# One more product step between the parts of a token tile's norm and transpose, in the out projection and the values of a Hymba layer

## The chip, the cores and the metric

The kernel runs on one core of a Trainium2 chip. Times are device microseconds (us) of one execution of the whole layer, lower is better. The core's engines are TensorE (PE, matrix products), VectorE (DVE), ScalarE (ACT), GpSimd (POOL) and SyncE (SP, which here only issues DMA transfers); each has its own instruction stream and runs it in order, and they meet through semaphores.

## The reference

The reference is one layer of a streaming encoder in float32, with 2048 tokens of width 1024. The pieces that lie around the change, cut to the core:

```python
y = concat([ya, yh]) @ w_out            # out projection
h = x + rms_norm(y, g_mix_post)         # h1
u = rms_norm(h, g_x_pre)
s = (u @ wq) . (m @ wk); p = softmax(s) # 4 heads, 256 memory tokens
y = (p . (m @ wv)) @ wo                 # values and output projection
h = h + rms_norm(y, g_x_post)           # h2
u = rms_norm(h, g_ffn_pre)
h = h + rms_norm((silu(u @ w_gate) * (u @ w_up)) @ w_down, g_ffn_post)
```

`rms_norm(a, g)` is `a / sqrt(mean(a*a) + eps) * g`, over the 1024 channels of a token.

## The kernel before

A first part of the kernel computes the in projection, the sliding window attention and the recurrence. After it, `phases()` (L1191) runs a list of jobs: the out projection, the scores, the values (in which the memory's value projection and the output matrix have been multiplied together beforehand), two jobs for the hidden half of the feed-forward network (FFN, for the first and second half of the tokens) and three for its down projection. In the out projection, the scores and the values a job is a row of eight blocks, and a block is two token tiles, n and n+1, of 128 tokens each. A block is one matrix product in the manner of Strassen: `seven` (L1114) makes it from seven product steps (numbered p = 1, 2, 5, 6, 7, 3, 4), each of which is twelve matmuls of 128x128 by 128x512: four pieces of the inner dimension times three (L1110 high part by high part, L1111 high by low, L1112 low by high). The first two and the last two blocks of a job are interleaved in pairs, step by step; the four between run alone. So the whole of `phases()` is one long row of product steps.

Each product step needs two operands as pairs of a rounded high part and a remainder: S, made from the tokens (`streamed`, `split2`: ACT or POOL rounds at L974 or L976, DVE subtracts at L977), and T, made from the weights or, for the FFN, from the norm's result (L974 with L977 on 128x1024). S is made about two steps ahead. T of the next job is loaded and split in halves, one half for each step.

After a step, results leave the banks of the accumulator: ACT copies (`part`, L1125; `row`, L1477) or DVE adds (L1475), and ACT squares each half with a sum (L1453). After the last step of a block, its token tiles' tail begins, written as a generator (`after()`, then `rest()`): at every product step that is issued, each live generator runs on to its next `yield`. So a `yield` is a distance of one product step in the program. The tail of a block of the values runs:

1. the reciprocal root of the mean square (`rstds`, POOL L1464, L1466, L1468), the scale by it and the gain (DVE L1584), a DMA on POOL that adds the residual to the row in place (`add`, L1482), and the store of the row to `h2_d` (SP, L78), one token tile per yield;
2. the squares of the sum (`mean_squares`, ACT L1453, called twice per tile), one tile per yield, and `rstds`;
3. the norm (DVE L1605) into a new row tile u, one tile per yield;
4. eight 128x128 transposes per tile on PE (L1364, into two banks), each half copied back into the row by ACT (L1365), and the store to `u_d`;
5. for tiles 4 to 7, sums and differences with the rows of the tiles 0 to 3 that are read back from `u_d`: one load `o`, four DVE operations (L1620, L1621, L1624, L1625) and four stores to `u_s` per tile. They become T of the FFN.

In the out projection (scale L1500) the tail is the same with the input x as residual, `h1_d`, no norm (its factor goes into the scores) and the transposes written in place over the row. For the last two blocks of a job (n of 12 or more) `rest()` runs beside the next job, on rows that are read back.

The Python order is not the order on the engines. A scheduler places every instruction, and may issue one ahead of where it was written, if its inputs allow. `behind()` (L1037) binds what is written inside it: it is issued after the last instruction that ACT, DVE, PE and SP each had when the current product step was written (`mark`, L1045). All row tiles (y, u, o, the sums, and the loads for T) share one ring of nine buffers (`row_tile`, L1435), and all loads and all stores of this part go through SP's one stream, in order: where an issue waits, those behind it wait as well.

## Time and profile before

| | us |
|---|---|
| median of 3 runs (lowest, highest) | 2555.17 (2553.72, 2556.72) |
| the profiled execution, its own time | 2553.45 |
| its span, first to last instruction | 2551.7 |
| PE busy in it | 2508.4 |
| DVE busy | 1759.2 |
| ACT busy | 1250.0 |
| POOL busy | 465.4 |

The profiled execution lies 1.72 us under the median. The out projection takes the stretch from 770 to 936 us of the span, the scores reach to 1102, the values to 1277, and the FFN's first product step follows there. Nearly all work on the other engines lies beside PE; where PE has a gap, the profile names what it waited for.

### The profile page before, as it was taken

The page shows a single profiled execution, that of the slowest core. Times are in us where ns is not written, and L with a number is a line of the kernel's source. Part 1 is how long each engine was busy: PE and PEld are TensorE (multiplying, and loading weights), DVE is VectorE, ACT ScalarE, POOL GpSimd, SP SyncE. Part 2 cuts the span into 40 slices and gives each one's busy share as a digit, 9 for nine tenths or more (in the row PEclk, how much of TensorE's full clock was granted, in tenths as well). Part 3 has the DMA queues.
Part 4 walks back from the last instruction along what each step waited for, and adds up shares of the span by engine and source line. Part 5 has one row for each costly group of instructions (what it writes and reads, how often), then busy time and mean ns, then how long its engine had stood idle before and what let it go on. Part 6 is the DMA issues. An engine that isn't in the chain of part 4 may idle for free.

```text
span 2551.7 us, 34118 instructions
## 1 busy us (share of the span) xinstructions
PE 2508.4 (98%) x12012; PEld 2091.8 (82%) x12012; DVE 1759.2 (69%) x2813; ACT 1250.0 (49%) x2606; POOL 465.4 (18%) x641
## 2 busy tenths in 40 slices
PE   8999999999999999999999999999999999999998
PEld 6777888887998888888788888888888888888886
DVE  6868588788667587787875655586666566664756
ACT  5454365556555566565554333353333344533543
POOL 2233343222323343224210000000000000000022
PEclk9999999999999999999999999999999999999999
DMA  6264545465996795858974542254555433666798
GB/s 239 97 209 133 176 142 164 153 200 186 283 310 225 217 281 198 283 194 241 313 229 129 180 146 75 99 182 141 182 197 193 161 129 131 206 208 196 221 226 206
DMA packets 269386, 489.97 MB, mean 192 GB/s; under 512 B 20640, under 2 KB 127136, under 8 KB 268704
## 3 DMA queue, kind: packets, MB, share of 16 engines
q1 hardware_dynamic: 255680, 439.57, 51.5%
q0 software_dynamic: 12384, 45.09, 8.9%
q10 hardware_dynamic: 1152, 3.15, 0.3%
q8 instruction: 94, 1.54, 0.2%
q14 instruction: 76, 0.62, 0.1%
HBM read 326.26 MB, written 161.48 MB: 191 GB/s over the span
## 4 chain that ended last, share of the span: by engine, by line
PE 89%; DMA 3%; DVE 2%; issue 2%; ACT 2%; POOL 1%; SPq 0%; POOLq 0%; DVEq 0%; ACTq 0%
PE psm L1110 23%; PE psm L1112 23%; PE psm L1111 23%; PE psg L170 3%; PE psg L172 3%; PE psg L171 3%; PE pss L1364 1%; DMA row<-h_d 1%; PE pss L824 0%; PE pst L824 0%; DMA sraw<-y_d 0%; PE psh L870 0%; PE psh L170 0%; PE psh L171 0%; PE psh L172 0%
## 5 line engine op out<-in xcount | busy, mean ns | idle before, releaser
L1110 PE MATMUL psm<-T,S 128*128 128x512 f32 x2744 | 1063.5, 392 | 12.1 <-ACT part L1125 5.4
L1111 PE MATMUL psm<-T,S 128*128 128x512 f32 x2744 | 1070.8, 390 | 0.0
L1112 PE MATMUL psm<-T,S 128*128 128x512 f32 x2744 | 1063.3, 391 | 3.2 <-DVE S L977 3.1
L1110 PEld LDWEIGHTS psm<-T,S 128*128 128x128 f32 x2744 | 516.0, 188 | 123.9 <-ACT part L1125 8.0
L1112 PEld LDWEIGHTS psm<-T,S 128*128 128x128 f32 x2744 | 516.0, 188 | 113.5 <-DVE S L977 5.7
L1111 PEld LDWEIGHTS psm<-T,S 128*128 128x128 f32 x2744 | 516.2, 188 | 106.2
L974 ACT ACTIVATE S<-sum 128x512 fp32r<-128x512 f32 (+1 forms) x336 | 206.2, 618 | 327.2 <-PE psm L1112 326.1
L977 DVE TENSOR_TENSOR S<-sraw,S 128x512 fp32r<-128x512 f32 (+1 forms) x312 | 211.7, 686 | 210.1 <-ACT S L974 195.0
L977 DVE TENSOR_TENSOR S<-sum,S 128x512 fp32r<-128x512 f32 (+1 forms) x400 | 271.6, 684 | 83.1 <-ACT S L974 65.5
L1125 ACT ACTIVATE part<-psm 128x512 f32<-128x512 f32 x294 | 173.1, 592 | 184.4 <-PE psm L1112 180.2
L974 ACT ACTIVATE S<-sraw 128x512 fp32r<-128x512 f32 (+1 forms) x271 | 165.7, 616 | 168.4 <-PE psm L1112 153.3
L1482 POOL DMA_DIRECT2D row<-y_d x28 | 25.1, 895 | 1072.2 <-DMA sraw<-hid_d 905.3
L170 PE MATMUL psg<-u,whi 128*128 128x512 f32 x352 | 142.6, 405 | 3.9 <-DVE z L696 2.1
L1453 ACT ACTIVATE junk<-row 128x512 f32<-128x512 f32 x160 | 99.6, 625 | 92.2 <-DVE row L1475 28.9
L977 DVE TENSOR_TENSOR T<-row,T 128x1024 fp32r<-128x1024 f32 x104 | 123.2, 1192 | 28.8 <-ACT T L974 28.4
L172 PE MATMUL psg<-u,wlo 128*128 128x512 f32 x352 | 142.0, 404 | 0.5 <-DVE wlo L153 0.5
L171 PE MATMUL psg<-u,whi 128*128 128x512 f32 x352 | 141.7, 403 | 0.0
L974 ACT ACTIVATE T<-row 128x1024 fp32r<-128x1024 f32 x104 | 105.3, 1023 | 20.2 <-DMA row<-in_w_down_dram 10.4
L1657 DVE TENSOR_TENSOR part<-psm,part 128x512 f32<-128x512 f32 x66 | 45.5, 689 | 66.6 <-PE psm L1112 66.4
L153 DVE TENSOR_TENSOR wlo<-raw,whi 128x1024 fp32r<-128x1024 f32 x54 | 68.1, 1263 | 29.0 <-ACT whi L150 18.4
L976 POOL TENSOR_SCALAR S<-sum 128x512 fp32r<-128x512 f32 x64 | 52.1, 814 | 174.1 <-PE psm L1112 142.4
L1648 DVE TENSOR_TENSOR row<-psm,part 128x512 f32<-128x512 f32 x66 | 45.5, 689 | 54.6 <-PE psm L1112 54.5
(343 smaller groups left out, 3472.4 us busy)
## 6 DMA issues: line engine op xcount, KB each, us to landing
sraw<-in_w_gate_dram SPq DMA_DIRECT2D x44, 512.0 KB, 5.0
sraw<-in_w_up_dram SPq DMA_DIRECT2D x44, 512.0 KB, 4.9
hid_d<-row SPq DMA_DIRECT2D x44, 512.0 KB, 2.7
h_d<-row SPq DMA_DIRECT2D x32, 512.0 KB, 7.0
y_d<-row SPq DMA_DIRECT2D x32, 512.0 KB, 4.2
sraw<-hid_d SPq DMA_DIRECT2D x32, 512.0 KB, 5.4
row<-h_d POOLq DMA_DIRECT2D x30, 512.0 KB, 7.4
row<-y_d POOLq DMA_DIRECT2D x28, 512.0 KB, 7.5
```

Of the source, the lines that this page charges most:

```text
L153: nc.vector.tensor_tensor(lo, raw, f32(hi), ALU.subtract)
L170: nc.tensor.matmul(ps, ah, bh, start=(i == 0), stop=False)
L171: nc.tensor.matmul(ps, ah, bl, start=False, stop=False)
L172: nc.tensor.matmul(ps, al, bh, start=False, stop=(i == n - 1))
L974: self.nc.scalar.activation(hi, raw, AF.Copy)
L976: self.nc.gpsimd.tensor_scalar(hi, raw, 1.0, 1.0, ALU.mult, ALU.mult)
L977: self.nc.vector.tensor_tensor(lo, raw, f32(hi), ALU.subtract)
L1110: nc.tensor.matmul(ps, s[:, 0, k, :], t[:, 0, k, :], start=st, stop=False, **kw)
L1111: nc.tensor.matmul(ps, s[:, 0, k, :], t[:, 1, k, :], start=False, stop=False, **kw)
L1112: nc.tensor.matmul(ps, s[:, 1, k, :], t[:, 0, k, :], start=False, stop=sp, **kw)
L1125: nc.scalar.activation(t, ps, AF.Copy)
L1453: self.nc.scalar.activation(junk, a, AF.Square, scale=float(D) ** -0.5, accum_out=to)
```

## The change

A product step more stands between the parts of a tile's tail: one `yield` more before the squares, for the early blocks and for the late ones; squares and transposes are written under `behind()`, so that the scheduler can no longer issue them ahead of their step; and in the values, one `yield` more between the norm and the transposes. No instruction, no transfer and no computed value is added or taken away.

```diff
--- before.py
+++ after.py
@@ -1503,6 +1503,7 @@
                 yield
             if n < NT - 4:
                 yield
+                yield
                 yield from rest()
 
         def rest():
@@ -1510,16 +1511,19 @@
             if n >= NT - 4:
                 for i in range(2):
                     y[i] = self.rows_of(self.h1_d, n + i)
-                for _ in range(3):
+                for _ in range(4):
                     yield
             for i in range(2):
-                self.mean_squares(y[i], i, s2)
+                with self.behind():
+                    self.mean_squares(y[i], i, s2)
                 yield
             r = self.rstds(s2)
             nc.gpsimd.tensor_scalar(self.r_x[:, n:n + 2], r, 1.0, None, ALU.mult)
             yield
             for i in range(2):
-                self.store(self.h1t_d[n + i], self.transposed(y[i], y[i]))
+                with self.behind():
+                    tv = self.transposed(y[i], y[i])
+                self.store(self.h1t_d[n + i], tv)
                 yield
 
         if n >= NT - 4:
@@ -1587,6 +1591,7 @@
                 yield
             if n < NT - 4:
                 yield
+                yield
                 yield from rest()
 
         def rest():
@@ -1594,10 +1599,11 @@
             if n >= NT - 4:
                 for i in range(2):
                     y[i] = self.rows_of(self.h2_d, n + i)
-                for _ in range(3):
+                for _ in range(4):
                     yield
             for i in range(2):
-                self.mean_squares(y[i], i, s2)
+                with self.behind():
+                    self.mean_squares(y[i], i, s2)
                 yield
             r = self.rstds(s2)
             u = [self.row_tile() for _ in range(2)]
@@ -1606,8 +1612,10 @@
                 yield
             o = []
             yield
+            yield
             for i in range(2):
-                tv = self.transposed(u[i], u[i])
+                with self.behind():
+                    tv = self.transposed(u[i], u[i])
                 self.store_transposed(self.u_d, n + i, tv)
                 if 4 <= n < 8:
                     o.append(self.row_tile().rearrange("p (k t) -> p k t", k=KT))
```

What this makes of the order shows on the engines. In the rows below a row names the line, the operation, what it writes and what it reads; the lines of the changed kernel have shifted by up to eight. The first place is ACT in the out projection, about where tiles 6 to 9 are squared and tile 6 is transposed. `row_1089` is tile 6, `row_1119` tile 7, `row_1097` and `row_1123` are tiles 8 and 9. Before:

```order
L1125 ACTIVATE part_1160_8547<-psm_1140_8452 128x512
L974 ACTIVATE S_1184_8646<-sraw_1139_8450 128x512
L1453 ACTIVATE junk_1163_8554,q_s_1157_8530<-row_1119_8337 128x512
L1365 ACTIVATE row_1089_8193<-pss_1178_8611 128x512
L1453 ACTIVATE junk_1164_8556,q_s_1157_8530<-row_1119_8337 128x512
L1365 ACTIVATE row_1089_8193<-pss_1179_8617 128x512
L1453 ACTIVATE junk_1166_8559,q_s_1165_8558<-row_1097_8221 128x512
L1453 ACTIVATE junk_1167_8561,q_s_1165_8558<-row_1097_8221 128x512
L974 ACTIVATE S_1205_8741<-sum_1204_8739 128x512
L1365 ACTIVATE row_1119_8337<-pss_1185_8649 128x512
```

And now:

```order
L1453 ACTIVATE junk_1166_8573,q_s_1160_8549<-row_1119_8337 128x512
L1453 ACTIVATE junk_1167_8575,q_s_1160_8549<-row_1119_8337 128x512
L1453 ACTIVATE junk_1169_8578,q_s_1168_8577<-row_1097_8221 128x512
L1453 ACTIVATE junk_1170_8580,q_s_1168_8577<-row_1097_8221 128x512
L1453 ACTIVATE junk_1171_8595,q_s_1148_8497<-row_1149_8498 128x512
L1453 ACTIVATE junk_1176_8607,q_s_1168_8577<-row_1123_8358 128x512
L974 ACTIVATE S_1212_8783<-sum_1211_8781 128x512
L1453 ACTIVATE junk_1177_8609,q_s_1168_8577<-row_1123_8358 128x512
L1477 ACTIVATE row_1163_8566<-psm_1140_8452 128x512
L1453 ACTIVATE junk_1178_8624,q_s_1148_8497<-row_1163_8566 128x512
L1365 ACTIVATE row_1089_8193<-pss_1180_8629 128x512
L1125 ACTIVATE part_1188_8666<-psm_1187_8653 128x512
```

The copies of the transposed tile 6 back into its row (L1365) stood between the squares of tile 7, and now stand behind the squares of tiles 7, 8 and 9.

The second place is PE in the values, at the transposes of tile 8, whose normed row is `row_2010` before and `row_2011` now. The `psm` tiles are the accumulators of two product steps, one after the other; before, the transposes cut into the first of them:

```order
L1111 MATMUL psm_2031_12680<-T_1695_11081,S_2020_12631 128x512
L1364 MATMUL pss_2027_12661<-ident_77,row_2010_12580 128x128 x4
L1364 MATMUL pss_2028_12667<-ident_77,row_2010_12580 128x128 x4
L1112 MATMUL psm_2031_12680<-T_1695_11081,S_2020_12631 128x512
L1110 MATMUL psm_2040_12718<-T_1695_11081,S_2026_12658 128x512
```

Now they stand behind both of them, and the product step that follows is the next one again:

```order
L1111 MATMUL psm_2036_12692<-T_1695_11081,S_2026_12652 128x512
L1112 MATMUL psm_2036_12692<-T_1695_11081,S_2026_12652 128x512
L1364 MATMUL pss_2042_12715<-ident_77,row_2011_12595 128x128 x4
L1364 MATMUL pss_2043_12721<-ident_77,row_2011_12595 128x128 x4
L1110 MATMUL psm_2046_12733<-T_1710_11156,S_2034_12687 128x512
```

Between the norm's place and the transposes there are 13 matmuls more than before: the last of the first step and all twelve of the second.

The third place is SP, and DVE with it, in the values, where tiles 4 and 5 are combined with tiles 0 and 1. Loads of `o` read `u_d`, stores of the sums go to `u_s0`, and `h2_d` takes the rows of tiles 6 and 7. SP before (`row_1935` and `row_1942` are the two `o`, `row_1884` and `row_1904` are tiles 6 and 7):

```order
L75 DMA row_1935_12233<-u_d_65 128x8x128
L75 DMA row_1942_12271<-u_d_65 128x8x128
L75 DMA sraw_1968_12390<-pt_d_60 128x2x512
L78 DMA u_d_65<-row_1914_12142 128x8x128
L78 DMA u_s0_4509<-row_1946_12292 512x1x128 x2
L75 DMA sraw_2014_12608<-in_w_gate_dram 128x2x512
L78 DMA u_d_65<-row_1915_12143 128x8x128
L78 DMA h2_d_62<-row_1884_12000 128x1024
L78 DMA h2_d_62<-row_1904_12107 128x1024
L78 DMA u_s0_4509<-row_1935_12233 512x1x128
L78 DMA u_s0_4509<-row_1957_12347 512x1x128 x2
```

And now (`row_1948` is the second `o`; tiles 6 and 7 are `row_1882` and `row_1899`; `row_1954` and `row_1972` hold the sums of tiles 4 and 5):

```order
L78 DMA u_d_65<-row_1916_12160 128x8x128
L78 DMA h2_d_62<-row_1882_11987 128x1024
L78 DMA h2_d_62<-row_1899_12089 128x1024
L75 DMA row_1948_12309<-u_d_65 128x8x128
L78 DMA u_s0_4509<-row_1954_12334 512x1x128 x2
L78 DMA u_d_65<-row_1917_12161 128x8x128
L78 DMA u_s0_4509<-row_1942_12275 512x1x128 x2
L78 DMA u_s0_4509<-row_1972_12402 512x1x128 x2
```

The second load of `o` and the first stores to `u_s0` stood ahead of the two stores to `h2_d`, and now stand behind them.

In the same place DVE has the norms of tiles 6 and 7 (L1605), S for the next product steps (L977), and the scales of tiles 8 and 9 (L1584). It had before:

```order
L1605 TENSOR_SCALAR row_1961_12356<-row_1884_12000,q_r_1960_12354,extra_1771_11458 128x1024
L1624 TENSOR_TENSOR row_1942_12271<-row_1942_12271,row_1957_12347 128x512
L1605 TENSOR_SCALAR row_1962_12357<-row_1904_12107,q_r_1960_12354,extra_1771_11458 128x1024
L1079 TENSOR_TENSOR sum_2060_12794<-sum_2044_12736,sraw_1966_12386 128x512
L977 TENSOR_TENSOR S_1994_12513<-sum_1993_12511,S_1994_12513 128x512
L1625 TENSOR_TENSOR row_1942_12271<-row_1942_12271 128x512
L977 TENSOR_TENSOR S_2001_12540<-sraw_1919_12166,S_2001_12540 128x512
L1079 TENSOR_TENSOR sum_2070_12827<-sraw_1965_12384 128x512
L1475 TENSOR_TENSOR row_1978_12435<-psm_1976_12421,part_1970_12405 128x512
L1584 TENSOR_SCALAR row_1929_12211<-row_1929_12211,q_r_1975_12416,g_1770_11456 128x1024
L1584 TENSOR_SCALAR row_1950_12312<-row_1950_12312,q_r_1975_12416,g_1770_11456 128x1024
```

And now (the norm is L1611, the scale L1588, the combination L1628 and L1629):

```order
L1628 TENSOR_TENSOR row_1972_12402<-row_1917_12161,row_1948_12309 128x512
L1629 TENSOR_TENSOR row_1972_12402<-row_1917_12161 128x512
L1611 TENSOR_SCALAR row_1963_12372<-row_1899_12089,q_r_1961_12369,extra_1771_11458 128x1024
L977 TENSOR_TENSOR S_1988_12483<-sum_1987_12481,S_1988_12483 128x512
L977 TENSOR_TENSOR S_1994_12517<-sraw_1919_12165,S_1994_12517 128x512
L1475 TENSOR_TENSOR row_1978_12429<-psm_1976_12415,part_1969_12395 128x512
L1632 TENSOR_TENSOR row_1948_12309<-row_1948_12309,row_1972_12402 128x512
L1588 TENSOR_SCALAR row_1929_12211<-row_1929_12211,q_r_1975_12410,g_1770_11456 128x1024
L1588 TENSOR_SCALAR row_1943_12289<-row_1943_12289,q_r_1975_12410,g_1770_11456 128x1024
```

The combination of tile 5 into `row_1972`, which was done before this stretch, now stands at its head, ahead of the norm of tile 7, of two S and of both scales.

## The prediction

> **What bounds the kernel now.** I read first how busy each engine is in the stretches that the change touches, by windows of time.
>
> ```profile
> core 0: us, PE busy (x) PEld busy (x) DVE busy (x) ACT busy (x) POOL busy (x), PEclk, DMA share, GB/s
> 740.00:960.00 220.00, 218.33 (x1035) 180.49 (x1034) 154.28 (x198) 124.86 (x258) 76.62 (x102) 1.00 0.80 247
> 960.00:1100.00 140.00, 140.00 (x682) 116.85 (x682) 108.41 (x194) 84.01 (x204) 37.24 (x55) 1.00 0.73 247
> 1100.00:1262.00 162.00, 157.24 (x738) 129.56 (x738) 126.31 (x178) 96.01 (x219) 57.20 (x75) 0.99 0.81 240
> 1220.00:1240.00 20.00, 18.41 (x91) 15.16 (x90) 13.02 (x19) 10.88 (x29) 7.21 (x10) 1.00 1.05 304
> 1240.00:1260.00 20.00, 17.27 (x76) 13.71 (x75) 15.54 (x21) 10.98 (x25) 5.22 (x9) 0.96 1.07 319
> 1262.00:1320.00 58.00, 58.00 (x266) 48.18 (x265) 50.09 (x66) 35.33 (x60) 9.95 (x11) 1.00 0.90 285
> ```
>
> PE has no gap in the scores and none after 1262; all that can be won lies in 1.67 us of idle time in the out projection (some of it ahead of the first tail) and 4.76 us in the values. The DMA share of about 1.05 in the last two fifths of the values says that the transfers there are as dense as they get, so they land late. Then I read PE's timeline for the single waits.
>
> ```profile
> 881.79 0.40 PE L1112 MATMUL psm<-T,S 128*128 128x512 f32 x1
> 879.91 0.66 PE L1364 MATMUL pss<-ident,row 128*128 128x128 f32 x4 [0.33 <-ACT row L1365]
> 882.50 0.50 PE L1110 MATMUL psm<-T,S 128*128 128x512 f32 x1 [0.31 <-ACT part L1125]
> 1174.13 0.50 PE L1110 MATMUL psm<-T,S 128*128 128x512 f32 x1 [0.44 <-ACT part L1125]
> 1236.84 0.39 PE L1111 MATMUL psm<-T,S 128*128 128x512 f32 x1
> 1238.83 1.06 PE L1364 MATMUL pss<-ident,row 128*128 128x128 f32 x8 [1.59 <-DVE row L1605]
> 1252.23 0.39 PE L1112 MATMUL psm<-T,S 128*128 128x512 f32 x1
> 1254.27 0.39 PE L1112 MATMUL psm<-T,S 128*128 128x512 f32 x1
> 1256.78 0.50 PE L1110 MATMUL psm<-T,S 128*128 128x512 f32 x1 [2.12 <-ACT S L974]
> 1258.12 0.54 PE L1112 MATMUL psm<-T,S 128*128 128x512 f32 x1 [0.61 <-DVE S L977]
> 1258.46 0.63 PE L1110 MATMUL psm<-T,S 128*128 128x512 f32 x1
> 1261.87 0.40 PE L1112 MATMUL psm<-T,S 128*128 128x512 f32 x1
> ```
>
> From 1252.23 to 1254.27 there are nine matmuls, 0.227 us each; that is the pace of an undisturbed step, 2.72 us for twelve. Against this pace 882.50 comes 0.48 us late, and with the 0.33 at 879.91 the out projection's transposes cost about 0.9 us. In the values the transposes of tile 8 wait 1.59 us for the norm, then one product step waits 2.12 and 0.61 us for its S, and from 1258.46 to 1261.87 eight matmuls start 0.43 us apart, which is half clock (PEclk 0.96 in that slice) and costs 8 x (0.43 - 0.227) = 1.6 us. With 0.44 us at 1174.13 all of it is 7.3 us, 0.3% of the time: the most that the change can win.
>
> What stands behind the waits of the values is the chain that ended last.
>
> ```profile
> 1198.50 0.90 POOL row L1482
> 1199.81 9.13 DMA row<-h_d
> 1222.26 11.12 DMA row<-h_d
> 1233.46 0.18 ACT junk L1453
> 1237.04 0.24 DVE row L1605
> 1244.13 1.29 DVE row L1584
> 1245.77 7.57 DMA row<-h_d
> 1253.44 1.34 ACT junk L1453 x4
> ```
>
> It is a tail feeding the next: scale (L1584), the add of the residual (L1482, 7.6 to 11.1 us until it lands), squares, norm, and on DVE the next tile's scale behind the norm. The S that PE awaits at 1256.78 is rounded by ACT right behind the squares at 1253.44, which began when the add of tile 10 had landed.
>
> **The change in the out projection.** ACT's timeline has the one long wait that the new order takes out.
>
> ```profile
> 876.33 0.60 ACT L1365 ACTIVATE row<-pss 128x512 f32<-128x512 f32 x1 [4.45 <-DMA h_d<-row]
> ```
>
> The copy of tile 6 writes over the row whose store to `h1_d` is still under way, and holds ACT's stream for 4.45 us; squares and part copies then crowd, and PE is late at 879.91 and 882.50. In the new order the squares of tiles 7 to 9 come first and the copy at least one product step (2.72 us) later, when the store has landed or nearly so. I take off 0.9 us. Bounds: nothing, if the two banks of the transposes are then late again, and 1.3 us, with one neighbouring delay of about 0.4. The wait at 1174.13 is for a part copy that stands late in both orders: unchanged.
>
> **The change in the values: the queue on SP.** These are the issues and DVE's rows that the order moves.
>
> ```profile
> 1194.12 0.98 SPq L75 DMA_DIRECT2D row<-u_d  x2
> 1206.16 3.45 SPq L78 DMA_DIRECT2D h_d<-row  x2
> 1209.70 6.67 SPq L78 DMA_DIRECT2D u_s<-row  x5
> 1207.42 0.68 DVE L1620 TENSOR_TENSOR row<-row,row 128x512 f32<-128x512 f32 x1
> 1219.43 2.47 DVE L1584 SCALAR_TENSOR_TENSOR row<-row,q_r,g 128x1024 f32<-128x1024 f32 x2
> 1233.02 0.69 DVE L1620 TENSOR_TENSOR row<-row,row 128x512 f32<-128x512 f32 x1 [4.67 <-DMA u_d<-row]
> u_s<-row SPq DMA_DIRECT2D x16, 256.0 KB, 6.3
> hid_d<-row SPq DMA_DIRECT2D x44, 512.0 KB, 2.7
> ```
>
> The stores of tiles 6 and 7 to `h2_d` can go only when the adds have landed, the second at 1199.81 + 9.13 = 1208.94, and SP is through them at 1206.16 + 3.45 = 1209.6. Before, both loads of `o` went at 1194.12. Now the second load and the stores of tile 4's sums stand behind: the load goes at 1209.6, two stores at about 1210.5 and 1211.6 (6.67 us for five, so 1.1 to 1.3 each), and with 6.3 us they have landed at about 1218. In the ring of nine rows the sums of tile 5 (`row_1972`) now get the place of the sums of tile 4, so DVE cannot combine tile 5 before 1218, where it did at 1207.42. Behind this in DVE's stream stand the norm of tile 7, two S and the scales of tiles 8 and 9. Counting DVE starts 0.6 us apart for 512 columns and 1.2 for 1024 (the rows above: two in 2.47), the two combinations, the norm, two S, an output sum and one more combination end at 1218 + 6 x 0.6 + 1.2 = 1222.8. So the scales start at 1222.8 and not at 1219.43: 3.4 us later. The bounds for this are -0.2 us, if the stores land in 2.7 us, as those to `hid_d` do in the FFN, and +8.1, if they land as slowly as the add's 11.12. I take 3.4, since 6.3 is the median of just these stores in just this stretch.
>
> The adds of tiles 8 and 9 then go 3.4 us later, the second at 1225.7; with the same 11.12 us it lands at 1236.8. From the squares at 1233.46 to the norm at 1237.04 it took 3.58 us, so the norm of tile 8 runs from 1240.4 to 1241.7.
>
> **PE at the transposes of tile 8.** The extra yield and `behind()` put them 13 matmuls later, 2.95 us: PE was there at 1236.84 + 0.23 = 1237.07, now comes at 1240.0, and waits 1.7 us for the norm: what is given is taken again by the queue, and the wait stays as it is. It is 0 with the norm in its old place, and up to 6 with the upper bound above.
>
> **The step that waits for S.** The norm of tile 8 ends at 1241.7. Then DVE has two combinations and two S (2.4 us), the norm of tile 9 (1.2) and one sum (0.6) ahead of the scale of tile 10, which so starts at 1245.9 and not at 1244.13: 1.8 us later. Its add lands 1.8 us later, at 1255.1, and ACT still has the squares of tile 10 ahead of that S. PE resumes at 1258.6. What PE lost or won before this is swallowed by the wait, except for what moves the chain itself: the 0.9 us of the out projection, which brings the whole of the values forward. So this term is +1.8, bounded by -4.3 (the waits of 1.59, 2.12 and 0.61 all gone) and by +6.5 (4.7 more from the upper bound above).
>
> **Half clock.** The trace shows a stretch of 8 matmuls at half clock after idle times of 2.12 and 0.61 us; after 1.59 us at 1238.83 it shows none. With a wait now of about 4.5 us (from 1254.1 to 1258.6), one such stretch is certain and a second one possible; I take half of one more, +0.8, bounds -1.6 and +1.6. The Trainium skill, in "TensorE: Matmul & The Clock Gate", section "What's actually happening", says that the clock goes to half after at least one idle window of about 3.4 us, a window that runs freely. The trace does not agree with the letter of it, since no idle time there reached 3.4; by the rule the longer wait would give one stretch where none was due before, and the sum would be +1.6 for this term in place of +0.8.
>
> **FFN.** The loads for its second T go behind two more stores to `h2_d`, which before were issued late.
>
> ```profile
> 1248.07 3.76 SPq L75 DMA_DIRECT2D row<-u_d  x2
> 1253.36 3.67 SPq L78 DMA_DIRECT2D h_d<-row  x2
> 1262.75 1.63 DVE L977 TENSOR_TENSOR T<-row,T 128x1024 fp32r<-128x1024 f32 x1
> ```
>
> They move from 1248.07 to about 1258.8 (1253.36 + 3.67 + 1.8), 10.7 us; the split on DVE from 1262.75 to at most 1273.5. The order has 60 matmuls and 16 transposes between 1262.1 and the FFN's first step, which with 0.227 and about 0.11 us (1.06 for eight, less overlap) is 1277.5, and the second T is used two steps later, at 1283. About 8 us remain: nothing, bounds 0 and +2.
>
> **Sum.** -0.9 + 1.8 + 0.8 = +1.7 us on the profiled execution's own 2553.45, so 2555.2; that execution lies 1.72 under the median of the runs, so 2556.9 for the median.
>
> **Rivals.**
> *The waits go, as the edit would have it:* the ring's row is free at about 1214.3, as with landings of 2.7 us, and the scales run 0.2 us earlier than before. The norm of tile 8 is then ready at about 1238, ahead of PE at 1240.0, and 1.59 us are saved. By the count above the scale of tile 10 starts 5.5 us behind the start of that norm, at 1242.3 in place of 1244.13, so S comes 1.8 us earlier; that PE finds it ready needs the add of tile 9 to land in 9.13 us, as the one at 1199.81 did, and not in 11.12. With both, 2.12 + 0.61 and the half clock of 1.6 go as well: -0.9 - 5.9 = -6.8, or 2548.4; with the first alone about 2552, as the chain would still end 2.7 us earlier. The DMA share of 1.05 speaks against both, and the order against it in that ACT's squares of tile 10 still stand ahead of that S.
> *The queue does more harm (this one ends slower):* the same row, released by SP's stores to `u_s0`, is free only at 1222.7, because they land like the add in 11.12 us. It decides from about 1221.5 on: then scales, adds, norm and S move by 4.7 us more, and PE waits for each in turn: 2556.9 + 4.7 = 2561.6. If the second pair (tiles 6 and 7, again behind the `h2_d` stores of tiles 8 and 9) is held up likewise, 2566. The DMA share speaks for it, and the 4.67 us that DVE waited for a row's store at 1233.02 already.
> *The change does nothing:* each wait comes back at the next consumer at its old size, 2555.2.
>
> **Chances.** What this kernel's measurement can tell from no change is about 0.2%, 5.1 us: 2550.1 to 2560.3. My sum has 0.37, the change that does nothing 0.09, and the first rival by its first condition alone 0.04: 0.5 for the same. Faster has 0.16, the first rival in whole. Slower has 0.34: the second rival 0.26, and 0.08 for my sum with its terms at their upper bounds, the FFN's T and a second half clock among them. The range holds the first rival's time and the second's worst: 2547.5 to 2566. The likeliest case alone has 2552 to 2560, which is its bounds of 0 to 1.3 in the out projection and one half clock more or less, with 2 us of landing time either way.
>
> **What would show it.** In the changed kernel's profile: ACT's wait for `h_d<-row` at a copy L1365 in 860 to 900 gone, and PE's two waits there; in the values DVE waiting at a combination (L1628) for `u_s<-row` at 1214 to 1218; the scales some 3 us later than 1219.4; PE waiting 1 to 2 us at the transposes of tile 8 and 4 to 5 us at the step that waits for S; a half clock stretch behind it; no wait in the FFN. I am wrong if DVE has its row in time, or if S is no longer behind squares that wait for an add.

## The result: slower by 0.36%, and the profile after

The changed kernel takes 2565.38 us (median of 6 runs, 2560.81 to 2567.25), the kernel before 2554.31 (6 runs, 2552.82 to 2556.72): the ratio is 1.0036, with an interval of 1.0026 to 1.0046. That is 11 us more. The profiled execution took 2562.21 us, with a span of 2560.2: 8.5 us over the span before, and 3.2 us under the median of its own runs.

PE's idle time by stretches, windows of the changed kernel:

```profile
core 0: us, PE busy (x) PEld busy (x) DVE busy (x) ACT busy (x) POOL busy (x), PEclk, DMA share, GB/s
740.00:960.00 220.00, 216.59 (x1036) 179.37 (x1035) 150.62 (x191) 123.19 (x251) 70.87 (x101) 1.00 0.79 243
960.00:1100.00 140.00, 139.01 (x676) 115.70 (x675) 110.07 (x197) 83.34 (x204) 40.89 (x55) 1.00 0.75 249
1100.00:1262.00 162.00, 157.91 (x748) 130.20 (x746) 125.28 (x178) 90.22 (x209) 54.28 (x73) 1.00 0.77 223
1262.00:1320.00 58.00, 54.62 (x235) 44.47 (x236) 48.91 (x62) 40.96 (x74) 12.19 (x15) 0.94 0.95 287
```

In 740 to 960 PE is now idle for 3.4 us (before 1.7), in the scores for 1.0 (before none), in the values for 4.1 (before 4.8) and in the start of the FFN for 3.4 (before none). The last two need care: the work has moved back against fixed windows, and the long wait that lay at 1256.78 now lies at 1265.10, on the other side of the border. The clock of 0.94 there is a stretch at half clock. PE's timeline has the single waits:

```profile
822.81 0.50 PE L1112 MATMUL psm<-T,S 128*128 128x512 f32 x1 [0.82 <-DVE S L977]
921.87 0.50 PE L1110 MATMUL psm<-T,S 128*128 128x512 f32 x1 [1.44 <-ACT S L974]
962.67 0.50 PE L1112 MATMUL psm<-T,S 128*128 128x512 f32 x1 [0.96 <-DVE S L977]
1228.40 0.50 PE L1110 MATMUL psm<-T,S 128*128 128x512 f32 x1 [2.85 <-ACT part L1125]
1248.03 1.03 PE L1364 MATMUL pss<-ident,row 128*128 128x128 f32 x8
1265.10 0.79 PE L1110 MATMUL psm<-T,S 128*128 128x512 f32 x1 [3.22 <-ACT S L974]
1265.69 0.63 PE L1111 MATMUL psm<-T,S 128*128 128x512 f32 x1
```

The two waits at 879.91 and 882.50 are gone, and so is the one of 1.59 us at the transposes of tile 8 (1248.03, no wait). Five have come or have grown: 0.82, 1.44 and 0.96 us from 822 to 963, 2.85 at 1228.40 and 3.22 at 1265.10. Two smaller ones are new at transposes, 0.35 us at 840.26 and 0.75 us at 1260.50. From 1265.69 to 1270.53 matmuls start 0.43 us apart, and there are about fourteen in the stretch from 1265.10, where before there were eight.

A fixed window hides how far the work has moved. Better marks are the first scale of the out projection (L1500), which comes ahead of anything that the change touches, and the first scale of the values. Each has one row that groups all scales of its line, with the start of the first and of the last. Before:

```profile
L1500 DVE SCALAR_TENSOR_TENSOR row<-row,q_r,g x16: 1270/1282/1667, 809.9 to 946.7; 128x1024 f32<-128x1024 f32 x16
L1584 DVE SCALAR_TENSOR_TENSOR row<-row,q_r,g x16: 1272/1278/1657, 1145.6 to 1289.2; 128x1024 f32<-128x1024 f32 x16
```

And now:

```profile
L1500 DVE SCALAR_TENSOR_TENSOR row<-row,q_r,g x16: 1271/1282/1667, 811.9 to 950.0; 128x1024 f32<-128x1024 f32 x16
L1588 DVE SCALAR_TENSOR_TENSOR row<-row,q_r,g x16: 1269/1275/1657, 1150.5 to 1300.9; 128x1024 f32<-128x1024 f32 x16
```

The first scale comes 2.0 us later than before, which no edit explains: it is what two executions differ by. From there to the first scale of the values it takes 338.6 us in place of 335.7, so the out projection and the scores lose 2.9. From there to the end of the span it takes 1409.7 in place of 1406.1, so the values and what follows lose 3.6. With the 2.0 ahead of them it is 8.5 in sum; so the profile puts 6.5 us to the stretches behind the first mark, of the 11 us between the medians, and the rest is not located. The same three marks are used for every run below.

In the values SP, DVE and ACT show how. SP's issues of the changed kernel, then DVE's rows, then ACT's:

```profile
1198.43 0.36 SPq L75 DMA_DIRECT2D row<-u_d  x1
1209.72 5.28 SPq L78 DMA_DIRECT2D h_d<-row  x2
1215.05 1.04 SPq L75 DMA_DIRECT2D row<-u_d  x1
1216.18 1.49 SPq L78 DMA_DIRECT2D u_s<-row  x2
```

```profile
1222.81 0.69 DVE L1628 TENSOR_TENSOR row<-row,row 128x512 f32<-128x512 f32 x1 [4.04 <-DMA u_s<-row]
1226.42 0.68 DVE L1475 TENSOR_TENSOR row<-psm,part 128x512 f32<-128x512 f32 x1
1227.62 2.48 DVE L1588 SCALAR_TENSOR_TENSOR row<-row,q_r,g 128x1024 f32<-128x1024 f32 x2
1241.78 0.69 DVE L1628 TENSOR_TENSOR row<-row,row 128x512 f32<-128x512 f32 x1 [6.20 <-DMA u_s<-row]
1258.45 0.68 DVE L1475 TENSOR_TENSOR row<-psm,part 128x512 f32<-128x512 f32 x1
```

```profile
1227.14 0.63 ACT L1453 ACTIVATE junk<-row 128x512 f32<-128x512 f32 x1 [4.93 <-DVE row L1475]
1227.77 1.07 ACT L1125 ACTIVATE part<-psm 128x512 f32<-128x512 f32 x2
1259.24 0.63 ACT L1453 ACTIVATE junk<-row 128x512 f32<-128x512 f32 x1 [2.33 <-DVE row L1475]
1264.42 0.63 ACT L974 ACTIVATE S<-sum 128x512 fp32r<-128x512 f32 x1
```

The first load of `o` goes at 1198.43, the second one at 1215.05, behind the two stores of tiles 6 and 7, and the stores of tile 4's sums at 1216.18. DVE can combine tile 5 only at 1222.81, after an idle 4.04 us for `u_s<-row`. The output sum (L1475) that stands behind it comes at 1226.42 and the scales at 1227.62. And here is what the prediction did not follow: ACT's stream has the square of that output sum ahead of two part copies. ACT is idle for 4.93 us until 1227.14, the part copies come at 1227.77, and PE waits 2.85 us for them. The second pair of tiles repeats it: DVE idle for 6.20 us at 1241.78, the output sum at 1258.45, ACT's square at 1259.24, and the S for which PE waits 3.22 us only at 1264.42.

### The profile page after: what moved, and what is told of

Same layout as the page of the kernel before. It is cut to its first block, busy times and chain, and to the rows that moved or that the text cites. A ratio compares the mean times of both kernels' runs of the same rounds, so it can differ in the third digit from the quotient of the medians.

```text
span 2560.2 us, 34120 instructions
## 1 busy us (share of the span) xinstructions
PE 2513.0 (98%) x12012; PEld 2094.5 (82%) x12012; DVE 1760.1 (69%) x2813; ACT 1249.6 (49%) x2606; POOL 462.5 (18%) x641
## 3 DMA queue, kind: packets, MB, share of 16 engines
q8 instruction: 94, 1.54, 0.2%
## 4 chain that ended last, share of the span: by engine, by line
PE 47%; issue 1%; DVE 1%; ACT 1%; DMA 1%; POOL 0%; DVEq 0%; POOLq 0%; ACTq 0%; SPq 0%
PE psm L1110 16%; PE psm L1112 16%; PE psm L1111 16%; DMA row<-u_s 0%; DMA u_d<-row 0%; ACT junk L1453 0%; DVE S L977 0%; ACT T L974 0%; PE pss L1364 0%; DVE row L1588 0%; ACT S L974 0%; ACT part L1125 0%; DVE row L1611 0%; DVE row L1723 0%; DVE sum L1079 0%
## 5 line engine op out<-in xcount | busy, mean ns | idle before, releaser
L977 DVE TENSOR_TENSOR S<-sraw,S 128x512 fp32r<-128x512 f32 (+1 forms) x312 | 211.0, 683 | 206.0 <-ACT S L974 190.4
L977 DVE TENSOR_TENSOR S<-sum,S 128x512 fp32r<-128x512 f32 (+1 forms) x400 | 271.1, 684 | 77.5 <-ACT S L974 60.8
L977 DVE TENSOR_TENSOR T<-row,T 128x1024 fp32r<-128x1024 f32 x104 | 123.4, 1193 | 32.5 <-ACT T L974 32.3
```

Source lines behind the costliest of these rows:

```text
L977: self.nc.vector.tensor_tensor(lo, raw, f32(hi), ALU.subtract)
```

## The experiments

The theory I began with: most of the loss comes of SP's queue in the values (the rival that ended slower), the out projection is nearly free. The first four runs take the change apart, by place and by kind.

**The out projection's part alone** (`mixed_block` as in the changed kernel, the values as before) and **the values' part alone** (`value_block` as changed, the out projection as before).

> The out projection's part of the change alone; the values are those of before. My theory: most of the loss is made in the values by SP's queue, and the out projection's part costs only what its own new waits in the profile add up to, some 3 us less 1.5 us of waits that went: +1 to +4 us, 2555.5 to 2558.5. A rival says that the loss comes from the out projection, which shifts all that follows against the loads: then +7 us or more.

> The part of the change in the values alone; the out projection is that of before. My theory: +6 to +10 us, 2560.5 to 2564.5, with the two waits of DVE at the combinations (L1620 in this kernel's lines or near it) for a store to u_s as in the changed kernel, 4 and 6 us. The rival of the out projection: under +3 us.

**The yields alone** (in both places the added `yield`s, no `behind()`) and **`behind()` alone** (in both places, no `yield` added):

```diff
-                with self.behind():
-                    self.mean_squares(y[i], i, s2)
+                self.mean_squares(y[i], i, s2)
```

```diff
                 yield
-                yield
                 yield from rest()
...
-                for _ in range(4):
+                for _ in range(3):
```

> All added yields, nothing under behind(). My theory: the yields move the second load of o and the stores to u_s behind the stores to h2_d, so this has most of the loss, +6 to +11 us, and DVE's two waits for u_s. The rival: what costs is behind(), because squares and transposes no longer fill gaps of ACT and PE; then under +3 us here.

> Squares and transposes under behind(), no yield added. SP's order in the values is that of before. My theory: within 3 us of before, no wait of DVE for u_s above 2 us. The rival of behind(): +6 us or more.

All runs, with the marks of their profiled executions. Each ratio is to runs of the kernel before made along with it, whose medians lie from 2554.05 to 2555.98 us, so the ratios compare better than the medians. The last two columns are the time from the first scale of the out projection to that of the values, and from there to the end, less that of before (335.7 and 1406.1). A stretch that an edit leaves as it was shows what this measure is good for: it came out from -1.2 to +1.6 us, and at +2.6 in one run, so single values under 3 us say little, the +2.9 of the whole change among them. The lower rows are the later experiments.

| kernel | median us | ratio to before, interval | out projection and scores | values and on |
|---|---|---|---|---|
| whole change | 2565.38 | 1.0036 (1.0026 to 1.0046) | +2.9 | +3.6 |
| out projection's part | 2562.50 | 1.0023 (1.0014 to 1.0032) | +8.6 | -1.0 |
| values' part | 2558.71 | 1.0009 (1.0001 to 1.0018) | +1.6 | +5.0 |
| yields alone | 2563.57 | 1.0029 (1.0018 to 1.0040) | +6.5 | +3.4 |
| `behind()` alone | 2562.77 | 1.0025 (1.0016 to 1.0034) | +5.2 | +3.2 |
| scores' T held back | 2571.59 | 1.0065 (1.0051 to 1.0078) | +15.9 | +0.6 |
| sums stored by ACT | 2560.26 | 1.0019 (1.0010 to 1.0028) | +1.6 | +7.3 |
| both, on the whole change | 2576.36 | 1.0082 (1.0068 to 1.0095) | +16.9 | +5.8 |
| out projection, early blocks | 2560.85 | 1.0027 (1.0016 to 1.0038) | +5.7 | -1.2 |
| out projection, last blocks | 2555.40 | 1.0010 (1.0001 to 1.0019) | +1.5 | +2.6 |
| T held for tile 10 alone | 2563.99 | 1.0043 (1.0031 to 1.0056) | +5.6 | +1.5 |
| `h2_d` stored by ACT | 2560.86 | 1.0025 (1.0014 to 1.0037) | -0.2 | +4.9 |
| the same, ring of ten | 2569.79 | 1.0054 (1.0042 to 1.0066) | +5.2 | +0.1 |

So my theory fell on two counts. The out projection's part costs at least as much as the values' part, and the yields or `behind()` alone cost nearly what both cost together; the parts do not add up. Of the expectations for `behind()` alone, that DVE waits for no store to `u_s` came true, and that it costs under 3 us did not. The out projection's part has no wait like those in the values. Its PE waits lie at its end and at the start of the scores:

```profile
919.17 0.50 PE L1110 MATMUL psm<-T,S 128*128 128x512 f32 x1 [1.79 <-ACT S L974]
954.76 0.50 PE L1112 MATMUL psm<-T,S 128*128 128x512 f32 x1 [0.75 <-DVE S L977]
961.36 0.50 PE L1112 MATMUL psm<-T,S 128*128 128x512 f32 x1 [1.31 <-DVE S L977]
966.34 0.77 PE L1110 MATMUL psm<-T,S 128*128 128x512 f32 x1 [2.40 <-ACT part L1125]
966.91 0.63 PE L1111 MATMUL psm<-T,S 128*128 128x512 f32 x1
```

With 0.98 us at 819.81 and 0.52 at 837.22 (start against the undisturbed pace), these are 8.4 us where before had 1.5; behind 966.34 come six matmuls at half clock, 1.3 us more. The same code cost less in the whole change's profile, +2.9, where only one of the three waits at the start of the scores is left (0.96 us): that place falls one way or the other, as is shown below.

**What makes the scores late: the order on SP?** In the changed kernel three loads for the scores' T (`row<-qk_d`) stand ahead of the store of tile 10, where before there were two, and with `behind()` alone four. The add of tile 11 then lands later: its store goes 10.4 us after the add's issue (908.52 to 918.95), where before it took 8.6 (906.06 to 914.62). ACT's squares of that tile stand ahead of the S that PE awaits at 919.17 above. Three runs try it. The first, on the out projection's part, ties these loads behind the latest store of an even tile; the second, on the values' part, has ACT issue the stores of the sums (`u_s`) in place of SP; the third is the changed kernel with both.

```diff
-                        half(g, self.row_tile)
+                        with self.tc.issue_after(self.h1_store):
+                            half(g, self.row_tile)
```

```diff
-                    self.store(self.u_s[c][:, :, at], t)
+                    self.put(self.u_s[c][:, :, at], t)
```

> The out projection's part alone, as in e1_mixed, but the loads for T of the scores (qk_d) are issued behind the store of tile 10 to h1_d, as before the change, instead of ahead of it. My theory: in the changed order two or three of these loads run beside the adds of tiles 10 and 11, which then land in 9 to 10.5 us instead of 7.9; their squares stand on ACT ahead of the S for which PE waits near 919. Then here the adds land in about 8 us, PE's wait near 919 is under 0.8 us in place of 1.8, and the time is 2 to 6 us under e1_mixed. The rival: the adds and the squares are late because of the yields and of behind() themselves, and the wait near 919 and the time stay as in e1_mixed, within 1.5 us.

> The values' part alone, as in e2_values, but the 16 stores of the sums to u_s are issued on ACT's queue; nothing else moves on PE, DVE and POOL. My theory of SP's queue: the stores no longer wait behind those to h2_d, so DVE's two waits for a store to u_s (4 and 6 us in the changed kernel) fall under 2 us, the scales start 3 us earlier or more, and the time falls by 2 to 5 us from e2_values, to 2554 to 2557. A first rival: the stores are slow since the transfers are dense, not since they are issued late; then DVE's waits stay above 3 us and the time stays. A second: ACT's stream is held up by the issues it now has, PE waits for S or part longer, and the time is that of e2_values or above.

> The whole change with both edits: loads for T of the scores held behind the store of tile 10, stores to u_s on ACT's queue. If these two orders on SP make the loss, it is gone here but for 1 or 2 us: 2554 to 2558, against 2565 of the change as it is. If the yields and behind() cost by themselves, it stays above 2561.

None won anything; the third took 2576.36 us, ratio 1.0082 (1.0068 to 1.0095). In the first, with the T held back, the adds of tiles 10 and 11 landed earlier, but ACT now waited for the T itself (3.96 us), and far longer for loads of `qk_s`, from which other operands of the scores are made and which had come behind the stores of tiles 12 to 15. ACT's row of it:

```profile
966.16 1.06 ACT L974 ACTIVATE T<-row 128x1024 fp32r<-128x1024 f32 x1 [17.31 <-DMA row<-qk_s]
```

PE paid 9.09 us for it at 970.87. In the second, with the sums stored by ACT, the second load of `o` still stood behind the `h2_d` stores, and DVE's first wait at a combination became one of 4.55 us for that load. Both edits moved a wait and did not take it away, so they told little about the cause. The next four were made sharper.

**The early blocks alone and the last two blocks alone** of the out projection (the condition is on `behind()` and on the added yields), **T held back for tile 10 alone**, and **the `h2_d` stores of the values issued by ACT**, right behind the squares that wait for the same add:

```diff
-                with self.behind():
+                with self.behind() if n < NT - 4 else contextlib.nullcontext():
                     self.mean_squares(y[i], i, s2)
```

```diff
                     self.mean_squares(y[i], i, s2)
+                    if n < NT - 4:
+                        self.put(self.h2_d[(n + i) * P:(n + i + 1) * P, :], y[i])
```

> The out projection's part of the change for its early blocks alone (tiles 0 to 11; the last two blocks and the values as before). SP's order up to the scores' start is that of the out projection's part. Theory Q (the loads of the scores' T stand ahead of a store that waits for an add): it alone costs +3 to +6 us, with PE waits at 915 to 925 and at 950 to 966 as with the whole part. Theory L (the squares and transposes of the last two blocks, which now stand later in ACT's stream beside the scores, do it): no cost here, within 2 us of before.

> The out projection's part for its last two blocks alone (tiles 12 to 15). SP's order is that of before up to the scores' middle. Theory Q: within 2 us of before, no PE wait of more than 1 us from 900 to 970. Theory L: +3 to +6 us.

> The out projection's part, with the loads of the scores' T tied behind the store of tile 10 alone (the earlier run tied others too, and the loads of the scores' rows came behind the stores of tiles 12 to 15 with a wait of 17 us). Theory Q: the adds of tiles 10 and 11 land at least 1 us earlier than the 9.1 us of that part, ACT's squares do not hold the S that PE needs at 919, the T loads now cost what they win: 2556 to 2562, and no wait of 9 us at 970. Theory L: like the out projection's part, 2562, with the same PE wait of about 2.4 us and half clock at 966.

> The values' part of the change, with the stores of tiles 0 to 11 to h2_d issued by ACT right behind each tile's squares, which wait for the same add; so neither the second load of o nor the stores of the sums stand behind them on SP. If SP's queue is what holds DVE in the values: no DVE wait of over 1 us at the first two combinations, the scales of tiles 8 and 9 start at 1218 to 1221 and not at 1227, the PE wait of 2.86 us for a part copy at 1223 falls under 1 us with its half clock stretch, and the time is 2 to 5 us under the values' part alone (2553 to 2557). If the queue is not what counts: 2558 to 2561, with the scales still at 1225 or later.

The early blocks carry the cost of the out projection's part: 1.0027 against 1.0010 for the last blocks, with +5.7 against +1.5 in that stretch. The last blocks' own squares and transposes, beside the scores, have at most a small share, as their interval (1.0001 to 1.0019) excludes 1 by little. But the order of T and stores on SP isn't either, or not alone: with T held for tile 10 only, no 9 us wait came, the store of tile 11 went 7.2 us after its add (10.5 in the out projection's part), and still the time was no better. ACT's rows of it show why:

```profile
917.87 1.06 ACT L974 ACTIVATE T<-row 128x1024 fp32r<-128x1024 f32 x1 [3.22 <-DMA row<-qk_d]
920.54 0.61 ACT L974 ACTIVATE S<-sum 128x512 fp32r<-128x512 f32 x1
```

The loads now go after the store, at 911.83 to 914.74, and ACT waits 3.22 us for the first; the S is ready at 921.15. This execution runs 1.9 us later than that of the out projection's part from its first scale on (810.8 and 808.9), so this is 919.2, where that part had it at 919.1: nothing is won. Ahead of the store they delay the adds, behind it they are late themselves. So whether the order on SP makes this one wait stays undecided: moving it exchanged one late transfer for another.

What is left, and weighs more in the profile of the out projection's part, is the start of the scores, where three of the six waits of the out projection's part lie with the half clock, 6.2 us of 9.7. There DVE and POOL get in each other's way, and which of the two pays differs between the next two kernels. DVE's rows before (two T splits, then the first maximum of the scores), and POOL's (two S, then the scaled maximum of 128x2):

```profile
947.93 2.35 DVE L977 TENSOR_TENSOR T<-row,T 128x1024 fp32r<-128x1024 f32 x2
955.01 1.27 DVE L1544 TENSOR_REDUCE x_mx<-row 128x2 f32<-128x512 f32 x2
```

```profile
948.93 4.23 POOL L976 TENSOR_SCALAR S<-sum 128x512 fp32r<-128x512 f32 x2
956.38 4.20 POOL L1546 TENSOR_SCALAR x_mr<-x_mx,r_x 128x2 f32<-128x2 f32 x1 [0.30 <-DVE x_mx L1544]
```

The same places with the early blocks alone:

```profile
949.90 4.23 DVE L977 TENSOR_TENSOR T<-row,T 128x1024 fp32r<-128x1024 f32 x2
957.65 0.67 DVE L1548 TENSOR_REDUCE x_mx<-row 128x2 f32<-128x512 f32 x1
```

```profile
950.30 1.61 POOL L976 TENSOR_SCALAR S<-sum 128x512 fp32r<-128x512 f32 x2
960.23 4.20 POOL L1550 TENSOR_SCALAR x_mr<-x_mx,r_x 128x2 f32<-128x2 f32 x1 [0.53 <-DVE x_mx L1548]
```

Before, DVE's two splits took 2.35 us and POOL's two S 4.23. With the early blocks' edits POOL's take 1.61 and DVE's 4.23. DVE's first maximum comes 2.6 us later and the second scaled maximum on POOL 3.9 (PE itself was late by about 1.1 us until then). But that DVE pays does not come of the edits alone: where the out projection is as before, DVE's splits took 3.62 us and POOL's two S 1.53 in the values' part alone, and 3.61 and 1.54 in the `h2_d` run, with PE waits of only 0.59 and 0.70 us there. What the edits have changed as well is the order on ACT. Before, and then with the early blocks alone:

```profile
958.25 0.58 ACT L1125 ACTIVATE part<-psm 128x512 f32<-128x512 f32 x1
960.61 0.60 ACT L1548 ACTIVATE row<-row,x_mr,r_x 128x256 f32<-128x256 f32 x1 [1.27 <-POOL x_mr L1546]
```

```profile
964.46 0.60 ACT L1552 ACTIVATE row<-row,x_mr,r_x 128x256 f32<-128x256 f32 x1 [2.50 <-POOL x_mr L1550]
965.64 0.57 ACT L1125 ACTIVATE part<-psm 128x512 f32<-128x512 f32 x1
```

Before, a part copy stands ahead of the second pair of exponentials, which waits for the second scaled maximum; now it stands behind this pair, and PE waits 2.42 us for it at 966.36. In these profiles the wait appears where the new order and the long scaled maximum of 4.20 us meet. The kernel before has the 4.20 us without the order, and no wait. The changed kernel, `behind()` alone and the run with T held for tile 10 have the order with a scaled maximum of 1.17 us, and no wait of 2.4 us. The out projection's part, its early blocks alone and the yields alone have both, and wait 2.40, 2.42 and 2.42 us. By the marks the three without this wait still lose 2.9, 5.2 and 5.6 us in that stretch, and the three with it 8.6, 6.5 and 5.7, so it is one part of the loss and not the whole. No run put ACT's order back or moved POOL's work away from there, so this is read from the rows and was not tried; what makes the rest of the out projection's loss stays open.

In the values the `h2_d` run took the queue away as meant. DVE's rows of it:

```profile
1204.59 0.68 DVE L1627 TENSOR_TENSOR row<-row,row 128x512 f32<-128x512 f32 x1
1216.76 0.69 DVE L1627 TENSOR_TENSOR row<-row,row 128x512 f32<-128x512 f32 x1 [3.04 <-DMA u_s<-row]
1221.57 2.47 DVE L1584 SCALAR_TENSOR_TENSOR row<-row,q_r,g 128x1024 f32<-128x1024 f32 x2
```

Tile 4 is combined at 1204.59 without a wait, and the second load of `o` is in time, but at tile 5 the next lock shows: the ring. Its sums take the row of tile 4's sums, whose stores are under way. The scales start at 1221.57, which is 77.3 us behind the first scale of the values, as in the values' part alone (77.2; before 73.8). PE waits 3.01 us for the same part copy, and the time is no better. The last run adds a tenth row to the ring, and pays for it with one of the six tiles that take the loads for S:

```diff
-        self.raws, self.parts, self.sums = 6, 4, 5
+        self.raws, self.parts, self.sums = 5, 4, 5
...
-name=f"row_{self._n}", bufs=9)
+name=f"row_{self._n}", bufs=10)
```

> The values' part, with the stores to h2_d behind the squares on ACT as in the run before, and a tenth row in the ring of row tiles (paid for with one of the six tiles that take the loads for S). The run before left one lock: DVE waited 2.41 and 3.04 us for rows whose stores were still under way, then the output sums, ACT's squares and its part copy came late, and PE waited 3.01 us at 1219. Theory R (the ring's row is the lock, SP's queue only sets how late it opens): no DVE wait of over 1 us at the norm of tile 7 and the combination of tile 5, scales of tiles 8 and 9 at 1218.5 to 1220 in place of 1221.6, the PE wait for the part copy under 1 us and no half clock behind it; time 3 us under the run before, 2554 to 2558, if the lost tile for loads costs nothing. Rival: the wait for the part copy comes of the yields' order on ACT itself, and stays at 2.5 to 3.2 us with the rows free; time as before, 2559 to 2562, or more if the lost tile costs.

As a whole it is the slowest but two, 2569.79 us: the missing tile costs, 6.7 us already ahead of the first scale of the out projection. The values themselves are told by the marks. Before the tenth row and with it:

```profile
L1584 DVE SCALAR_TENSOR_TENSOR row<-row,q_r,g x16: 1267/1275/1669, 1144.3 to 1295.1; 128x1024 f32<-128x1024 f32 x16
```

```profile
L1500 DVE SCALAR_TENSOR_TENSOR row<-row,q_r,g x16: 1271/1282/1651, 816.6 to 957.7; 128x1024 f32<-128x1024 f32 x16
L1584 DVE SCALAR_TENSOR_TENSOR row<-row,q_r,g x16: 1270/1280/1672, 1157.5 to 1306.4; 128x1024 f32<-128x1024 f32 x16
```

From the first scale of the values to the end of the span (2555.3 and 2563.7) it takes 1411.0 and 1406.2 us. The latter is before's 1406.1. The view of DVE's waits by what ended them, from 1140 to 1270 (us in total, times, the longest), has as its largest for a transfer with nine rows:

```profile
DVE row L1627 <- DMA u_s<-row: 9.6, 2, 6.5
```

and with ten:

```profile
DVE sum L1079 <- DMA sraw<-pt_d: 7.2, 3, 3.4
```

```profile
1234.29 0.50 PE L1110 MATMUL psm<-T,S 128*128 128x512 f32 x1 [1.69 <-ACT part L1125]
```

No wait for the stores of the sums is left (the whole change has 10.2 us of it, the values' part alone 8.5, before none). In its place DVE waits for the loads for S, for which a tile is missing, so the scales come hardly earlier, 76.0 us behind the first. PE's wait for the part copy falls from 3.01 to 1.69 us, with no half clock behind it; under 1 us, as expected, it did not, and a wait of 4.07 us for S at 1270.84 stays. So the locked row of the ring is what DVE waits for in the values, with SP's queue as a second lock in front of it. That this is the whole of the 5 us is not shown: the missing tile changes the stretch too, and the 1406.2 us are one execution. Nor is it the only way to lose there: `behind()` alone has SP's order of before and no wait of DVE for `u_s`, and still costs 3.2 us by the marks, with PE waits of 2.74 us at 1262.99 and of 0.54 and 1.61 us in the FFN (1302.32 and 1306.49).

## Why the prediction was right or wrong, point by point

The time lies in the range, and the likeliest case, no measurable change, was wrong. The outcome is that of the rival that ended slower, but not by its condition: the row of the ring was free when I had forecast it, and not 4.7 us later. That the median of 2565.38 us lies so near to the 2566 of that rival's worst case is luck in good part: the loss in the out projection and the scores was in none of its terms.

- *The queue on SP and the ring.* Right in place and in size. All in the values has moved by the 4.9 us of the first scale. Less these, DVE combines tile 5 at 1217.9 (predicted 1218), the scales start at 1222.7 (1222.8), the second add goes at 1230.46 - 4.9 = 1225.6 (1225.7).
- *PE at the transposes of tile 8.* Predicted 1.7 us of waiting, measured none. PE had been held before them. The transposes of tile 9 waited instead, 0.75 us at 1260.50: ACT copied those of tile 8 out of their banks only at 1259.87, behind squares that had waited for output sums.
- *What waits for the output sum.* This is the step that failed. I counted DVE's stream behind the late combination, with the output sum in it, and went on to the scales and the adds. I did not ask who waits for that output sum: ACT's square, and behind it the part copies of a running product step. That is 2.85 us on PE at 1228.40, where the prediction had 0, and it came in the values' part alone at the same size (2.86).
- *The step that waits for S.* I had +1.8 us, anchored to the add of tile 10. PE resumes at 1265.10 - 4.9 = 1260.2 in place of 1256.78, so +3.4. The chain into it was again the output sum behind a late combination (DVE idle 6.20 us), which I had only as a worst case of the slower rival. PE's wait itself was 3.22 us and not about 4.5; that figure ran from 1254.1, where the rows I showed have PE's last matmul end at 1254.27 + 0.39 = 1254.66, which would have left about 3.9.
- *Half clock.* +0.8 predicted; six matmuls more at 0.2 us are +1.2.
- *The out projection.* The sign of this term was wrong. The wait of ACT for `h_d<-row` and PE's waits at 879.91 and 882.50 went as said, worth 0.9. I did not look at what the tails had filled, nor past the tails into the scores. The transposes of tile 0, which before ran from 819.41 to 820.2, had covered a wait for S that is now idle time (0.82 us at 822.81); the S behind tile 11's squares (1.44 at 921.87), one more at the start of the scores (0.96 at 962.67) and 0.35 us at 840.26 are the rest that PE's rows show. The whole is +2.9 in the profiled execution, and the part alone costs 1.0023 by its median.
- *The scores and the FFN at nothing.* The scores lose 1.0 us in their window, which is the wait of 0.96 us just named; one more wait of 0.28 us came in the FFN, and one of 1.63 us in the values' part alone, within the bounds given.
- *The rival that the change does nothing.* Refuted: the whole is slower than before by an interval that excludes 1, and so is either half of it, by place or by kind, though the values' part only just (1.0001).

## What to carry to other kernels

When an instruction is forecast to start late on an engine, list everything behind it on that engine, and for each of these the engine that waits for it and what stands behind there; the scale that I followed was harmless, the output sum ahead of it was not. In a row of product steps that runs with 1% of idle time, a moved piece of work has usually been filling something, and its old place has to be priced like its new one. Where two locks stand one behind the other, opening one measures as nothing; and the time between two marks inside the kernel, with stretches that no edit touches as the measure of chance, tells more than the end of the run.

## What the runs showed of the hardware that was not expected

A subtraction on DVE with both inputs in SBUF and a rounding on POOL that run side by side slow each other: two 128x1024 splits took 2.35 us on DVE in one kernel and 4.23 in another, and two 128x512 roundings on POOL 4.23 and 1.61 in the same two. A scaled maximum of 128x2 on POOL took 0.29, 1.17 or 4.20 us. The Trainium skill, in "SBUF — State Buffer", section "Who interferes with whom", says that a DVE instruction with two SBUF inputs contends with a GpSimd instruction that reads SBUF, and that the order of issue decides which one blocks. The trace agrees that the two meet. Which one pays cannot be told from the starts in these rows: POOL's first rounding starts 1.00 us behind DVE's first split in the kernel before, where POOL pays (4.23), and 1.00 us behind it in the `h2_d` run, where DVE does (3.61); in the changed kernel they share it, with 3.17 us on DVE and 3.25 on POOL.

Half clock does not follow from the length of the idle time alone. After 2.40 us at 966.34 in the out projection's part there is a stretch of it (the row at 966.91 above, 0.63 us); in the early blocks alone, after 2.42 us at the same place, there is none. PE's rows of the latter:

```profile
966.36 0.47 PE L1110 MATMUL psm<-T,S 128*128 128x512 f32 x1 [2.42 <-ACT part L1125]
966.67 0.39 PE L1111 MATMUL psm<-T,S 128*128 128x512 f32 x1
```

In the changed kernel the 2.85 us at 1228.40 left none, where 2.86 us in front of the same product step in the values' part alone left a stretch of about nine matmuls. Whether a stretch comes must be put as a chance.
